# Seven block products for half of the first FFN's down projection, woven between its gate and up products

## The chip, the cores and the metric

The kernel runs on one core of a Trainium2 chip. TensorE (PE) multiplies, VectorE (DVE) and ScalarE (ACT) do the work around the products, GpSimd (POOL) a few small things, and SyncE (SP) issues nearly all transfers from HBM. The metric is the device time of one execution in microseconds, the median over runs; less is better.

## The reference, cut to what matters

A decoder trunk of two layers works on 256 tokens of width 1024, in float32. Each layer is FFN, mixer, FFN; each FFN has 2816 hidden columns and adds half of its result.

```python
def swiglu(x, w_gate, w_up, w_down):
    return (jax.nn.silu(x @ w_gate) * (x @ w_up)) @ w_down

for layer in range(DEPTH):
    h = h + 0.5 * swiglu(rms_norm(h, ffn1_norm[layer]), ...)
    hn = rms_norm(h, mix_norm[layer])
    h = h + (ab_mixer(hn, ...) if layer % 2 == 0 else c_mixer(hn, ...))
    h = h + 0.5 * swiglu(rms_norm(h, ffn2_norm[layer]), ...)
return rms_norm(h, final_norm)
```

The change touches one FFN of the four, the first of layer 0 (`ffn(0)`).

## The kernel before, in words

Everything is kept transposed: a tile holds 128 columns of the model or of the hidden width on its partitions and the 256 tokens along the free axis. A float32 product is made of three matmuls (`mm3`, lines 354 to 356) of parts in fp32r: high x high, high x low, low x high. So each operand is first split into two parts, by a copy on ScalarE (`hi`) and a subtraction on VectorE (`lo`). For x and h that is done once; for the weights it is done for every chunk.

The weights come as one stream of chunks of up to 128 x 2048 floats (1 MB). `weight_chunks` writes their order down, and the class `Stream` runs it: SP loads a chunk into one of 3 raw buffers (line 183), ACT copies it into `whi` (line 231), DVE subtracts into `wlo` (line 238), usually in two halves of 1024 elements, and there are 4 buffers of `whi` and `wlo`. A load may start when the chunk three before it has been split, a split when TensorE is done with the chunk four before it (`room`, `pump`). `SHIFT` puts a chunk 16 elements into its buffer where the weights are the stationary operand; chunks whose weights move have no shift.

An FFN goes through 22 hidden tiles in 11 pairs. Pair p has a gate chunk and an up chunk, called Gp and Up here: 256 hidden columns each, 48 matmuls of 256 columns, one PSUM bank each. After that `gated` makes h of the pair: DVE multiplies the gate by the row of 1/rms (`gs`, line 684), ACT takes silu (line 685), DVE multiplies by up (`hm`, line 687), and `split` makes `hTh` and `hTl` (line 359). In `ffn(0)` the row is made late, from the sums of squares that are formed during the first chunks (lines 446 to 458), and the first two pairs are gated together after G2 (`late = 4`). The down projection then runs for four groups of 256 columns, each in three chunks of 8, 8 and 6 hidden tiles (`DOWN`), with the weights stationary and h moving; after each group `nxt.pair` adds it to x, makes the next stage's x parts, and squares.

The program's order is not the final order on each engine: a planner goes through it and issues on each engine the earliest instruction in program order that its own model of the machine holds to be ready. Queues are then fixed and in order. PSUM has 8 banks.

The last FFN (`ffn(5)`) already makes its down projection by seven block products (Strassen's scheme in Winograd's form) for 9 of its pairs, with h stationary (`hTh`, and sums `hSh`) and 512 weight columns moving.

Of the kernel before, what the change touches and what calls it, by code (L numbers as in the profile page):

```python
# [10 lines left out]
F32 = mybir.dt.float32  # L11
# [34 lines left out]
SPARE = 2  # L46
AHEAD = [(phase, n) for phase in (2, 3) for n in (4, 8, 12, 16)] + [(3, 19)]

MIX1, MIX2 = (4, 5, 6, 7, 0, 1, 2, 3), (0, 1, 2, 3, 4, 5, 6, 7)


def weight_chunks():

    chunks = []

    def add(m, r, n, c0, c1, shift=0, cuts=(), reset=0, summed=False, kind="N"):
        chunks.append((m[:-1], m[-1], r, n, c0, c1, shift, cuts, reset, summed, kind))

    def cols(m, c0, w, cuts=(), reset=0):
        n = CH // w  # L60
        for k in range(0, KD, n):
            add(m, k * 128, n, c0, c0 + w, SHIFT if w == 256 else 0, cuts, reset)

    def ffn(name, layer, last=False, again=(2, 3)):
        first = len(chunks)
        for c in range(0, FF, 256):
            if len(chunks) == 0:
                for k in (0, 4):
                    add((f"{name}_w_gate", f"{name}_w_up", layer), k * 128, 4, c, c + 256, SHIFT,
                        (1, 2, 3) if k else (0.5, 1, 1.5, 2, 3))  # L70
                continue
            for m in ("gate", "up"):
                n = len(chunks)
                cuts = (6,) if first == 0 and n in again else ()
                cols((f"{name}_w_{m}", layer), c, 256, cuts, RESET if n - first in again else 0)
        wd = (f"{name}_w_down", layer)
        if last:
            for i in range(FT // 2):
                add(wd, i * 256, 2, 0, D, kind=LAST[i])
            return  # L80
        for c in range(0, D, 256):
            for k, n in DOWN:
                add(wd, k * 128, n, c, c + 256, SHIFT)

    def mix(m, order, summed=False):
        for k in order[:4:2]:
            add(m, k * 128, 2, 0, D, SHIFT)
        for c in (0, 512):
            add(m, order[4] * 128, 4, c, c + 512, SHIFT, summed=summed and c == 0)

    ffn("ffn1", 0, again=(2,))
    wab = ("ab_w_in", 0)
    cols(wab, 0, 256)
    cols(wab, 512, 256, reset=RESET)
    cols(wab, 1024, 512)
    cols(wab, 2048, 512)
    for c, n in ((1536, RESET), (1792, 0), (256, RESET), (768, RESET)):
        cols(wab, c, 256, reset=n)
    mix(("ab_w_out", 0), MIX1)
    ffn("ffn2", 0, again=(2,))  # L100
    ffn("ffn1", 1, again=())
    wc = ("c_w_in", 0)
    for c in range(4):
        cols(wc, c * 256, 256, reset=RESET if c % 2 else 0)
        cols(wc, 1024 + c * 256, 256, reset=0 if c else RESET)
        if c % 2 == 0:
            cols(wc, 2048 + c * 256, 512)
    mix(("c_w_out", 0), MIX2, True)
    ffn("ffn2", 1, True, again=(2,))
    return chunks  # L110
# [17 lines left out]
class Stream:  # L128
# [12 lines left out]
    def add(self, nk, w, shift, cuts, reset, summed, kind):  # L141

        cuts = (*(cuts or (() if reset else (nk / 2,))), nk)
        j = self.chunks
        self.chunks += 1
        for step in (1, 2) if kind != "N" else (0,):
            if step < 2 or kind == "X":
                if step == 1 and self.wide is None:
                    self.wide = len(self.loads)
                self.loads.append((j, nk, w, loads_of(j), step))  # L150
            self.specs.append((len(self.loads) - 1, j, nk, w, shift, cuts, reset, summed, step, kind))
# [48 lines left out]
    def split_parts(self):  # L200
        u = self.split
        nc = self.nc
        r, j, nk, w, shift, cuts, reset, summed, step, kind = self.specs[u]
        formed = kind == "Z" and step == 1
        raw = self.raws[r] if formed else self.raws.pop(r)
        his, los = (p.tile([128, CH + LINE], F32R, name=m) for p, m in ((self.hi_pool, "whi"), (self.lo_pool, "wlo")))

        h = w // 2
        far = nk * w - reset * h + RESHIFT // LINE * LINE + RESHIFT

        def at(k):
            return int(k * w) - reset * h + shift

        def part(t, k):
            if k >= reset:
                return t[:, at(k) : at(k) + w]
            return Halves(*(t[:, a : a + h] for a in (far + k * h, shift + k * h)))

        self.parts[u] = tuple([part(t, k) for k in range(nk)] for t in (his, los))

        def split(a, r):
            n = r.free_size()
            hi, lo = his[:, a : a + n], los[:, a : a + n]
            if len(r.shape) == 3:
                hi, lo = (t.rearrange("p (k c) -> p k c", k=reset) for t in (hi, lo))
            if self.lead:
                done = nc.vector.tensor_copy(hi, r)
                self.lead()
                self.lead = None
            else:  # L230
                done = nc.scalar.activation(hi, r, AF.Copy)  # L231
            if summed:
                nc.scalar.activation(lo, r, AF.Copy, scale=-1.0)
                src = self.weights[j, : 128 * nk * w].rearrange("(p c) -> p c", p=128)
                c0 = a - shift
                nc.gpsimd.dma_start(lo, src[:, c0 : c0 + n], accum_op=ALU.add)
            else:
                self.made[u] = done, nc.vector.tensor_sub(lo, r, hi.bitcast(F32))  # L238

        if step:  # L240
            q = w // 2
            self.parts[u] = tuple([t[:, i * q : (i + 1) * q] for i in range(4)] for t in (his, los))
            split(0, raw[:, : 2 * q])
            if formed:
                to = raw[:, : 2 * q].rearrange("p (i c) -> p i c", i=2)
                t2 = raw[:, 2 * q : 3 * q]
                first = nc.vector.tensor_sub(to, t2.unsqueeze(1).to_broadcast([128, 2, q]), to)
            yield
            if formed:
                with self.tc.issue_after(first.ins):  # L250
                    split(2 * q, raw[:, 2 * q :])
                nc.vector.tensor_sub(t2, t2, raw[:, 3 * q :])
            else:
                end = 4 * q if step == 1 else 3 * q
                split(2 * q, raw[:, 2 * q : end])
            yield
            self.read += not formed
            self.split += 1
            return
        if reset:  # L260
            r = raw[:, : reset * w].rearrange("p (k c) -> p k c", k=reset)
            split(far, r[:, :, :h])
            split(shift, r[:, :, h:])
        k0 = reset
        for k1 in cuts:
            split(at(k0), raw[:, int(k0 * w) : int(k1 * w)])
            k0 = k1
            yield
        self.read += 1
        self.split += 1  # L270
# [41 lines left out]
def trunk(ctx: ExitStack, tc: tile.TileContext, a, out):  # L312
# [340 lines left out]
    def ffn(phase):  # L653
        nonlocal nxt
        with tc.tile_pool(name="fp", bufs=1) as fp:
            hT = [fp.tile([128, FT, S], F32R, name=n) for n in ("hTh", "hTl")]
            last = phase == 5
            if last:
                size = [128, len(SEVEN), 3, 128]
                early = [fp.tile(size, t, name=n) for t, n in ((F32, "hSh"), (F32R, "hSl"))]  # L660
# [21 lines left out]
            def gated(k, pg, pu):  # L682
# [6 lines left out]
                if seven:  # L689
# [6 lines left out]
                    nc.vector.tensor_sub(a21, a12, s2)  # L696
                    nc.vector.tensor_scalar(a22, a22, -1.0, None, op0=ALU.mult)
                split(hT[0][:, k : k + 2], hT[1][:, k : k + 2], hm)
                if seven:
                    split(*(h[:, SEVEN.index(k // 2)] for h in hS), f[:, :3])  # L700

            late = {0: 4, 3: 2}.get(phase, 3)
            if phase in (2, 5):
                split(*parts[:2], nxt.acc[:, 0])
            for n in range(FT):
# [34 lines left out]
                        gated(i, *ready[i : i + 2])  # L740
                elif n > late and m == 1:
                    gated(k, *ready[-2:])
            if last:
                wide = [xp.tile([128, KD, S], F32, name=m).rearrange("p k s -> p (k s)") for m in ("xTh", "xTl")]
                st.spare.append(wide[0])
# [2 lines left out]
                return  # L748
            row = norm["half"]
            nxt = Next(phase + 1)  # L750
            for c in range(4):
                b = bank()
                for k0, n in DOWN:
                    w = st.take()
                    for kk in range(n):
                        k = k0 + kk
                        for j in range(2):
                            cs = slice(j * 128, (j + 1) * 128)
                            mm3(b[:, j * S : (j + 1) * S], w[0][kk][:, cs], w[1][kk][:, cs], hT[0][:, k], hT[1][:, k],
                                k == j == 0, k == FT - 1 and j == 1)  # L760
                    if k0 + n == FT:
                        nxt.pair(c, b, row, fp)
                    st.free()

    def finish(hT, hS, half, away, xr, xn, fg):

# [539 lines left out]
def _layout(a):  # L1306
# [6 lines left out]
    for j, (ms, layer, r, n, c0, c1, *how) in enumerate(chunks):  # L1313
# [2 lines left out]
            w = w[:, ROWS]  # L1316
        w = tiles(w)
        if how[-1] != "N":
            w = w.reshape(128, 4, -1)[:, [3, 1, 0, 2]]
        w = w.reshape(128, loads_of(j), -1).transpose(1, 0, 2)  # L1320
        weights[j, : w.size] = w.ravel()
    norms = np.stack([a[n] for n in ("ffn1_norm", "mix_norm", "ffn2_norm")]).reshape(-1, 128)
# [34 lines left out]
```

## Time and profile before

| | us |
|---|---|
| median of 3 runs | 924.01 (923.49 to 924.04) |
| span of the profiled execution, first to last instruction | 922.4 |
| the profiled execution's own time beyond its span | not given; the runs' median is 1.6 above the span |
| PE busy | 915.0 (99%) |
| DVE busy | 689.8 (75%) |
| ACT busy | 528.4 (57%) |
| first FFN on PE, up to the first product of the mixer | 185.8 |
| of that, its down projection | 125.95 to 185.79 |

Rows of a timeline give start, length, engine, line and operation, output and inputs, shapes, a count (x2 where rows were merged), and in brackets the idle time before it on its engine and what ended it. PE is pipelined: a matmul takes longer than the distance to the next one's start.

### The profile page before, as it was taken

The page shows a single profiled execution, that of the slowest core. Times are in us where ns is not written, and L with a number is a line of the kernel's source. Part 1 is how long each engine was busy: PE and PEld are TensorE (multiplying, and loading weights), DVE is VectorE, ACT ScalarE, POOL GpSimd, SP SyncE. Part 2 cuts the span into 40 slices and gives each one's busy share as a digit, 9 for nine tenths or more (in the row PEclk, how much of TensorE's full clock was granted, in tenths as well). Part 3 has the DMA queues.
Part 4 walks back from the last instruction along what each step waited for, and adds up shares of the span by engine and source line. Part 5 has one row for each costly group of instructions (what it writes and reads, how often), then busy time and mean ns, then how long its engine had stood idle before and what let it go on. Part 6 is the DMA issues. An engine that isn't in the chain of part 4 may idle for free.

```text
span 922.4 us, 18258 instructions
## 1 busy us (share of the span) xinstructions
PE 915.0 (99%) x7583; PEld 896.5 (97%) x7583; DVE 689.8 (75%) x1058; ACT 528.4 (57%) x808; POOL 80.8 (9%) x117
## 2 busy tenths in 40 slices
PE   9999999999999999999999999999999999999997
PEld 9999999999999999999999999999999999999886
DVE  7976556587888867655677666667778799978897
ACT  7754444468667545444564444455776777555574
POOL 0000000033310000000000000001565100000002
PEclk9999999999999999999999999999999999999999
DMA  9765554665256677766556878865533466855681
GB/s 325 272 228 183 180 195 174 228 226 181 93 183 230 220 281 266 296 238 218 187 209 236 305 272 313 318 216 192 184 137 137 119 230 225 277 191 206 223 310 60
DMA packets 33985, 202.15 MB, mean 219 GB/s; under 512 B 3904, under 2 KB 6208, under 8 KB 12528
## 3 DMA queue, kind: packets, MB, share of 16 engines
q1 hardware_dynamic: 32400, 197.79, 59.8%
q0 software_dynamic: 496, 1.77, 0.9%
q10 hardware_dynamic: 1008, 1.44, 0.5%
q8 instruction: 59, 0.97, 0.4%
q14 instruction: 22, 0.18, 0.1%
HBM read 188.14 MB, written 12.85 MB: 218 GB/s over the span
## 4 chain that ended last, share of the span: by engine, by line
PE 93%; issue 4%; DMA 2%; POOL 0%; DVE 0%; ACT 0%; POOLq 0%; DVEq 0%
PE bank L354 30%; PE bank L355 30%; PE bank L356 30%; DMA raw<-in_weights 1%; PE bank L1059 1%; DMA x<-blocks 1%; PE bank L601 1%; DMA xTl<-away 0%; POOL xTl L803 0%; DVE wlo L238 0%; PE bank L604 0%; PE bank L1021 0%; PE bank L1023 0%; PE bank L1022 0%; PE bank L1208 0%
## 5 line engine op out<-in xcount | busy, mean ns | idle before, releaser
L231 ACT ACTIVATE whi<-raw 128x1024 fp32r<-128x1024 f32 (+5 forms) x349 | 331.6, 994 | 280.4 <-issue 154.6
L238 DVE TENSOR_TENSOR wlo<-raw,whi 128x1024 fp32r<-128x1024 f32 (+5 forms) x349 | 390.6, 1149 | 78.8 <-ACT whi L231 77.8
L354 PE MATMUL bank<-xTh,whi 128*128 128x256 f32 x1600 | 442.7, 277 | 0.0
L356 PE MATMUL bank<-xTh,wlo 128*128 128x256 f32 x1600 | 441.8, 276 | 0.0
L355 PE MATMUL bank<-xTl,whi 128*128 128x256 f32 x1600 | 441.8, 276 | 0.0
L355 PEld LDWEIGHTS bank<-xTl,whi 128*128 128x128 f32 x1600 | 300.4, 188 | 0.0
L354 PEld LDWEIGHTS bank<-xTh,whi 128*128 128x128 f32 x1600 | 300.4, 188 | 0.0
L356 PEld LDWEIGHTS bank<-xTh,wlo 128*128 128x128 f32 x1600 | 300.4, 188 | 0.0
L356 PE MATMUL bank<-hTh,wlo 128*128 128x256 f32 x528 | 145.7, 276 | 0.0
L354 PE MATMUL bank<-hTh,whi 128*128 128x256 f32 x528 | 145.7, 276 | 0.0
L355 PE MATMUL bank<-hTl,whi 128*128 128x256 f32 x528 | 145.7, 276 | 0.0
L355 PEld LDWEIGHTS bank<-hTl,whi 128*128 128x128 f32 x528 | 99.1, 188 | 0.0
L354 PEld LDWEIGHTS bank<-hTh,whi 128*128 128x128 f32 x528 | 99.1, 188 | 0.0
L356 PEld LDWEIGHTS bank<-hTh,wlo 128*128 128x128 f32 x528 | 99.1, 188 | 0.0
L687 DVE TENSOR_TENSOR hm<-gs,bank 128x512 f32<-128x512 f32 x44 | 29.9, 683 | 45.4 <-PE bank L356 44.4
L954 POOL MEMSET k<- 64x256 f32 x12 | 3.2, 307 | 565.2 <-ACT whi L231 378.9
L684 DVE TENSOR_TENSOR gs<-bank,row 128x512 f32<-128x512 f32 x44 | 30.1, 686 | 21.3 <-PE bank L356 21.1
L354 PE MATMUL bank<-mixh,whi 128*128 128x256 f32 x128 | 35.7, 279 | 0.0
L356 PE MATMUL bank<-mixh,wlo 128*128 128x256 f32 x128 | 35.4, 277 | 0.0
L355 PE MATMUL bank<-mixl,whi 128*128 128x256 f32 x128 | 35.4, 276 | 0.0
L1050 POOL TENSOR_SCALAR pr<-pr,rl 128x128 f32<-128x128 f32 (+1 forms) x36 | 31.9, 899 | 29.5 <-DVE rl L1046 20.5
L359 ACT ACTIVATE hTh<-hm 128x512 fp32r<-128x512 f32 x44 | 27.1, 619 | 8.8 <-DVE hm L687 8.0
(231 smaller groups left out, 994.1 us busy)
## 6 DMA issues: line engine op xcount, KB each, us to landing
raw<-in_weights SPq DMA_DIRECT2D x139, 1024.0 KB, 5.0
raw<-in_weights SPq DMA_DIRECT2D x12, 768.0 KB, 4.8
blocks<-in_weights SPq DMA_DIRECT2D x9, 1024.0 KB, 10.0
blocks<-blocks SPq DMA_DIRECT2D x9, 1024.0 KB, 8.7
raw<-blocks SPq DMA_DIRECT2D x7, 1024.0 KB, 4.8
raw<-in_weights SPq DMA_DIRECT2D x6, 512.0 KB, 6.6
raw<-in_weights SPq DMA_DIRECT2D x7, 256.0 KB, 5.7
blocks<-block SPq DMA_DIRECT2D x5, 256.0 KB, 8.9
```

Source lines behind the costliest of these rows:

```text
L231: done = nc.scalar.activation(hi, r, AF.Copy)
L238: self.made[u] = done, nc.vector.tensor_sub(lo, r, hi.bitcast(F32))
L354: nc.tensor.matmul(p, sh, mh, start=start, stop=False)
L355: nc.tensor.matmul(p, sh, ml, start=False, stop=False)
L356: return nc.tensor.matmul(p, sl, mh, start=False, stop=stop)
L359: return nc.scalar.activation(hi, src, AF.Copy), nc.vector.tensor_sub(lo, src, hi.bitcast(F32))
L601: nc.tensor.matmul(o, w[0][i][:, cs], xT[m][:, k], start=k == 0 and m == "h" and j % 2 == 0, stop=False)
L684: nc.vector.tensor_mul(g, both(pg), twice(norm["row"]))
L687: nc.vector.tensor_mul(hm, g, both(pu))
L954: nc.gpsimd.memset(pair[j][o, 1].bitcast(F32), 0.0)
L1050: share = engine.tensor_scalar(pr[:, cs], pr[:, cs], rl[:, b : b + 1], None, op0=ALU.mult)
L1059: nc.tensor.transpose(tp[:, i * 128 : (i + 1) * 128], pr[:, i * 128 : (i + 1) * 128], ident)
```

## The change

For the first FFN (`WOVEN = (0,)`), columns 0 to 511 of the down projection are made by seven block products per pair of h tiles. The pair's h (2 hidden tiles x 256 tokens) is cut into 2 x 2 blocks by hidden tile and by half of the tokens, its weights (2 x 512) into 2 x 2 blocks of 256 columns, and seven products of a block or a sum of blocks replace eight. Called S0 to S10 here, they are woven into the stage: Sp stands behind U(p+2) (`LAG = 2`), S9 behind S8 and S10 behind the first chunk of the third column group. In them h is stationary and the weights move; the seven sums stay in four PSUM banks from S0 to S10.

- The weights of Sp come as one chunk of 128 x 1024 floats, kind `"S"`, put 48 elements into the buffer (`MSHIFT`). DVE forms four sums of blocks in the unused half of the raw buffer (three instructions), and ACT and DVE split seven blocks instead of four.
- `gated` also forms four sums of h blocks on DVE (three instructions) and splits them (`hSh`, `hSl`, three buffers).
- After S10, `gather_first` adds the seven results up into four quarters, with one ACT copy and seven DVE instructions. They have tokens on the partitions, so `turned` transposes them on PE (four 128 x 128 blocks at a time) into a bank, after the second and third chunk of the third group, and hands them to `nxt.pair`. The groups of columns 512 to 1023 are as before.

```diff
+WOVEN = (0,)
+LAG = 2
+MSHIFT = 48
@@ weight_chunks
+        def seven(pair):
+            add(wd, pair * 256, 2, 0, 512, MSHIFT, kind="S")
...
+            if woven and c // 256 >= LAG:
+                seven(c // 256 - LAG)
...
-        for c in range(0, D, 256):
+        rest = list(range(FT // 2 - LAG, FT // 2)) if woven else []
+        if woven:
+            seven(rest.pop(0))
+        for c in range(512 if woven else 0, D, 256):
             for k, n in DOWN:
                 add(wd, k * 128, n, c, c + 256, SHIFT)
+                if rest:
+                    seven(rest.pop(0))
@@ Stream.split_parts
+        if kind == "S":
+            q = w // 2
+            self.parts[u] = tuple([t[:, shift + i * q : shift + (i + 1) * q] for i in range(7)] for t in (his, los))
+            b12, t13, t1, t2, t4 = (raw[:, i * q : j * q] for i, j in ((0, 1), (4, 6), (4, 5), (6, 7), (7, 8)))
+            split(shift, raw[:, q : 4 * q])
+            nc.vector.tensor_add(t13.rearrange("p (i c) -> p i c", i=2),
+                                 raw[:, q : 3 * q].rearrange("p (i c) -> p i c", i=2),
+                                 b12.unsqueeze(1).to_broadcast([128, 2, q]))
+            nc.vector.tensor_add(t2, t1, raw[:, 2 * q : 3 * q])
+            nc.vector.tensor_add(t4, t2, raw[:, 3 * q : 4 * q])
+            yield
+            split(shift + 3 * q, raw[:, 4 * q :])
...
@@ gated
+                if woven:
+                    f = g.rearrange("p i (t c) -> p (i t) c", t=2)
+                    a11, a12 = (hm[:, i, :128] for i in range(2))
+                    nc.vector.tensor_sub(f[:, :2], hm[:, 0].rearrange("p (t c) -> p t c", t=2), hm[:, :, 128:])
+                    nc.vector.tensor_sub(f[:, 2], f[:, 1], a11)
+                    nc.vector.tensor_add(f[:, 3], a12, f[:, 2])
+                    summed[k // 2] = [fp.tile([128, 4, 128], F32R, name=m, bufs=3) for m in ("hSh", "hSl")]
+                    split(*summed[k // 2], f)
@@ ffn
+            def seven_products(c):
+                if not sevens:
+                    sevens.extend(bank() for _ in range(4))
+                w = st.take()
+                plain = [[h[:, 2 * c + k, t * 128 : (t + 1) * 128] for h in hT] for k, t in ((0, 0), (1, 0), (1, 1))]
+                s3, s1, s2, s4 = ([h[:, i] for h in summed[c]] for i in range(4))
+                a11, a12, a22 = plain
+                for i, (at, (sh, sl), q) in enumerate(((0, a11, 0), (1, a12, 2), (2, s4, 1), (3, a22, 6), (4, s1, 3),
+                                                       (5, s2, 5), (6, s3, 4))):
+                    b = sevens[at // 2][:, at % 2 * S : (at % 2 + 1) * S]
+                    mm3(b, sh, sl, w[0][q], w[1][q], c == 0 and at % 2 == 0, c == FT // 2 - 1 and at in (1, 3, 5, 6))
+                st.free()
+                summed.pop(c)
...
+            def gather_first():
+                p1, p2, q3, q4, q5, p6, p7 = (sevens[i // 2][:, i % 2 * S : (i % 2 + 1) * S] for i in range(7))
...
+                nc.scalar.activation(u1, p1, AF.Copy)
+                nc.vector.tensor_add(u2, u1, p6)
+                nc.vector.tensor_add(c11, u1, p2)
+                nc.vector.tensor_add(u3, u2, p7)
+                nc.vector.tensor_add(c21, u3, q4)
+                nc.vector.scalar_tensor_tensor(c22, u3, -1.0, q5, op0=ALU.mult, op1=ALU.add)
+                nc.vector.scalar_tensor_tensor(v, u2, -1.0, q5, op0=ALU.mult, op1=ALU.add)
+                nc.vector.tensor_add(c12, v, q3)
...
+            def turned(i, parts):
+                b = bank()
+                for j in range(2):
+                    for t in range(NT):
+                        at = j * S + t * 128
+                        nc.tensor.transpose(b[:, at : at + 128], parts[t][:, j * 128 : (j + 1) * 128], ident)
+                nxt.pair(i, b, norm["half"], fp)
...
+                if woven and m == 1 and k // 2 >= LAG:
+                    seven_products(k // 2 - LAG)
...
+            rest = list(range(FT // 2 - LAG, FT // 2)) if woven else []
+            if woven:
+                seven_products(rest.pop(0))
-            for c in range(4):
+            for c in range(2 if woven else 0, 4):
...
+                    if woven and c == 2 and k0:
+                        turned(k0 // 16, quarters[k0 // 16])
                     if k0 + n == FT:
                         nxt.pair(c, b, row, fp)
                     st.free()
+                    if rest:
+                        seven_products(rest.pop(0))
+                        quarters = gather_first()
```

More of the change, by code (lines that the diff above doesn't have):

```diff
@@ L62, in cols, with ffn @@
             add(m, k * 128, n, c0, c0 + w, SHIFT if w == 256 else 0, cuts, reset)
-    def ffn(name, layer, last=False, again=(2, 3)):
+    def ffn(name, layer, last=False, again=(2, 3), woven=False):
         first = len(chunks)
+        wd = (f"{name}_w_down", layer)
+        def seven(pair):
+            add(wd, pair * 256, 2, 0, 512, MSHIFT, kind="S")
         for c in range(0, FF, 256):
@@ L75, in ffn @@
                 cols((f"{name}_w_{m}", layer), c, 256, cuts, RESET if n - first in again else 0)
-        wd = (f"{name}_w_down", layer)
+            if woven and c // 256 >= LAG:
+                seven(c // 256 - LAG)
         if last:
@@ L89, in mix @@
             add(m, order[4] * 128, 4, c, c + 512, SHIFT, summed=summed and c == 0)
-    ffn("ffn1", 0, again=(2,))
+    ffn("ffn1", 0, again=(2,), woven=0 in WOVEN)
     wab = ("ab_w_in", 0)
@@ L99, in weight_chunks @@
     mix(("ab_w_out", 0), MIX1)
-    ffn("ffn2", 0, again=(2,))
-    ffn("ffn1", 1, again=())
+    ffn("ffn2", 0, again=(2,), woven=2 in WOVEN)
+    ffn("ffn1", 1, again=(), woven=3 in WOVEN)
     wc = ("c_w_in", 0)
@@ L145, in add @@
         self.chunks += 1
-        for step in (1, 2) if kind != "N" else (0,):
+        for step in (1, 2) if kind in "ZX" else (0,):
             if step < 2 or kind == "X":
@@ L238, in split @@
                 self.made[u] = done, nc.vector.tensor_sub(lo, r, hi.bitcast(F32))
+        if kind == "S":
[10 more added lines that the diff above has]
+            split(shift + 3 * q, raw[:, 4 * q :])
+            yield
+            self.read += 1
+            self.split += 1
+            return
         if step:
@@ L657, in ffn @@
             last = phase == 5
+            woven = phase in WOVEN
             if last:
@@ L699, in gated @@
                 if seven:
                     split(*(h[:, SEVEN.index(k // 2)] for h in hS), f[:, :3])
+            summed, sevens = {}, []
+            def seven_products(c):
[11 more added lines that the diff above has]
+                summed.pop(c)
@@ new lines, in gather_first @@
+            def gather_first():
+                p1, p2, q3, q4, q5, p6, p7 = (sevens[i // 2][:, i % 2 * S : (i % 2 + 1) * S] for i in range(7))
+                t = [fp.tile([128, 2, S], F32, name="gs", bufs=2) for _ in range(2)]
+                t += [fp.tile([128, 2, S], F32, name="hm", bufs=2) for _ in range(2)]
+                (u1, u2), (u3, v), (c11, c21), (c12, c22) = ([v[:, i] for i in range(2)] for v in t)
+                nc.scalar.activation(u1, p1, AF.Copy)
[6 more added lines that the diff above has]
+                nc.vector.tensor_add(c12, v, q3)
+                sevens.clear()
+                return (c11, c21), (c12, c22)
@@ L1318, in _layout @@
         if how[-1] != "N":
-            w = w.reshape(128, 4, -1)[:, [3, 1, 0, 2]]
+            w = w.reshape(128, 4, -1)[:, [1, 0, 3, 2] if how[-1] == "S" else [3, 1, 0, 2]]
         w = w.reshape(128, loads_of(j), -1).transpose(1, 0, 2)
```

## The prediction

> **What bounds the kernel now.** I read the profile page first (shares by engine, then the chain of work that ended last), next the table of stages for the first FFN, and then the timelines of PE, DVE and ACT in that stage.
>
> ```profile
> span 922.4 us, 18258 instructions
> PE 915.0 (99%) x7583; PEld 896.5 (97%) x7583; DVE 689.8 (75%) x1058; ACT 528.4 (57%) x808; POOL 80.8 (9%) x117
> PE 93%; issue 4%; DMA 2%; POOL 0%; DVE 0%; ACT 0%; POOLq 0%; DVEq 0%
> ```
>
> ```profile
> 16.80:28.00 11.20, 11.20 (x101) 11.20 (x100) 10.56 (x14) 9.36 (x14) 0.00 (x0) 1.00 0.82 292
> 28.00:49.80 21.80, 21.80 (x195) 21.80 (x194) 20.26 (x25) 15.53 (x20) 0.00 (x0) 1.00 0.78 283
> 49.80:125.95 76.15, 76.15 (x674) 76.15 (x673) 47.32 (x51) 35.60 (x43) 0.00 (x0) 1.00 0.56 197
> 125.95:185.80 59.85, 59.85 (x531) 59.85 (x530) 36.06 (x42) 27.42 (x35) 0.00 (x0) 1.00 0.53 190
> ```
>
> The chain is TensorE for 93% of the span. In the table of stages the columns are stretch, length, then busy us (and instructions) of PE, PEld, DVE, ACT and POOL, the granted clock, the DMA share and GB/s. From 16.8 to 185.8 us PE is busy for the whole of every stretch, at clock 1.00. So in this FFN a matmul less is time less, as long as nothing else becomes late. DVE is the one to watch: busy 20.26 of 21.80 us from 28.0 to 49.8, only 47.32 of 76.15 in the rest of the gate and up products, 36.06 of 59.85 in the down projection. GpSimd does nothing here.
>
> A busy PE need not be at its peak, so I take its pace from starts.
>
> ```profile
> 27.69 0.28 PE L356 MATMUL bank<-xTh,wlo 128*128 128x256 f32 x1
> 27.80 0.28 PE L446 MATMUL bank<-acch,all_ones 128*128 128x256 f32 x1
> 27.92 0.28 PE L447 MATMUL bank<-accl,all_ones 128*128 128x256 f32 x1
> 28.03 0.28 PE L354 MATMUL bank<-xTh,whi 128*128 128x256 f32 x1
> ...
> 125.95 0.28 PE L354 MATMUL bank<-hTh,whi 128*128 128x256 f32 x1
> ...
> 185.79 0.28 PE L354 MATMUL bank<-xTh,whi 128*128 128x256 f32 x1
> ```
>
> The first row of the down projection starts at 125.95 and the first of the mixer at 185.79. Between them are 22 h tiles x 8 column tiles x 3 matmuls = 528: 59.84/528 = 0.1133 us each, with no gap. One chunk of a gate or up product (48 matmuls) takes 5.44 us: those of pair 2 (G2, U2) run from 28.03 to 38.91, and G3, U3 to 49.8.
>
> **The change part by part.**
>
> *Fewer products (PE).* Half the columns cost 22 x 4 x 3 = 264 matmuls of 256 columns before; now 11 pairs x 7 products x 3 = 231, also of 256 columns. 33 x 0.1133 = -3.74 us. PE changes between the two kinds of stream some 22 times; the rows at 27.80 and 28.03 show such a change, with steps of 0.11 and 0.12, so I take nothing for it.
>
> *Pace of the new products.* In them h is stationary and the weights move. The kernel has such products of 256 columns in its last stage only.
>
> ```profile
> 911.71 0.39 PE L356 MATMUL bank<-whi,hTl 128*128 128x512 f32 x1
> 911.94 0.39 PE L354 MATMUL bank<-whi,hTh 128*128 128x512 f32 x1
> ...
> 913.65 0.28 PE L354 MATMUL bank<-whi,hTh 128*128 128x256 f32 x1
> ...
> 916.05 0.28 PE L356 MATMUL bank<-whi,hTl 128*128 128x256 f32 x1
> ```
>
> ```profile
> 217.81 0.66 PE bank L1059 x6
> ```
>
> From 913.65 to 916.05 are 20 steps of 0.120, not 0.1133, though the 512-column ones keep 0.23 (2 x 0.1133 is 0.227). So the pace depends on something other than shape. Ends for 231 matmuls: 0 and 231 x 0.0067 = +1.55 us. The unshifted weights of the tail start at offset 0 of their buffer; the products above that run at 0.1133 read weights 16 elements further (SHIFT), and the new ones are put 48 further (MSHIFT). As offset is the difference I can see, I take 0. TensorE: Matmul & The Clock Gate in the Trainium skill (Step-by-step, LDWEIGHTS) says that loading the next weights doesn't take read bandwidth from the running matmul, so that one shape would have one pace and this term could only be 0; the tail's 0.120 disagrees, which is why I keep the upper end.
>
> *Turning the sums back.* Eight 128x128 transposes are new, in two groups of four. The chain has six of L1059's in 0.66 us (last row above): 0.11 each, +0.88 us.
>
> *VectorE: weights.* ACT and DVE split every chunk into two parts.
>
> ```profile
> 36.03 1.23 DVE L238 TENSOR_TENSOR wlo<-raw,whi 128x1024 fp32r<-128x1024 f32 x1 [0.67 <-ACT whi L231]
> 37.17 0.42 DVE L452 SCALAR_TENSOR_TENSOR sqrt<-sqrt,mean 128x256 f32<-128x256 f32 x1
> 37.51 1.22 DVE L238 TENSOR_TENSOR wlo<-raw,whi 128x1024 fp32r<-128x1024 f32 x1
> 38.64 0.42 DVE L454 SCALAR_TENSOR_TENSOR row<-sqrt,inverse 128x256 f32<-128x256 f32 x1
> 39.09 1.29 DVE L684 TENSOR_TENSOR gs<-bank,row 128x512 f32<-128x512 f32 x2
> 40.50 1.23 DVE L238 TENSOR_TENSOR wlo<-raw,whi 128x1024 fp32r<-128x1024 f32 x1
> 42.44 1.28 DVE L687 TENSOR_TENSOR hm<-gs,bank 128x512 f32<-128x512 f32 x2 [0.72 <-ACT gs L685]
> 43.64 0.69 DVE L684 TENSOR_TENSOR gs<-bank,row 128x512 f32<-128x512 f32 x1
> 44.24 1.22 DVE L238 TENSOR_TENSOR wlo<-raw,whi 128x1024 fp32r<-128x1024 f32 x1
> 45.38 1.28 DVE L359 TENSOR_TENSOR hTl<-hm,hTh 128x512 fp32r<-128x512 f32 x2
> ...
> 47.18 1.22 DVE L238 TENSOR_TENSOR wlo<-raw,whi 128x1024 fp32r<-128x1024 f32 x1
> 48.32 0.68 DVE L359 TENSOR_TENSOR hTl<-hm,hTh 128x512 fp32r<-128x512 f32 x1
> 48.92 1.21 DVE L238 TENSOR_TENSOR wlo<-raw,whi 128x1024 fp32r<-128x1024 f32 x1
> ```
>
> From start to start: 1.14 for 1024 elements (44.24 to 45.38), 0.60 for 512 (43.64 to 44.24), 0.34 for 256 (37.17 to 37.51); by the same slope about 0.87 for 768 and 0.21 for 128. An S chunk (one pair's share of 512 columns) costs three sums (512, 256, 256: 1.28) and splits of 768 and 1024 (2.01): 3.3 us of DVE. A pair's h sums cost 0.34 + 0.21 + 0.21 and a split of 512, 0.60: 1.36 us. ACT gets three copies more, under 2.5 us per pair, beside 35.60 busy of 76.15.
>
> In the steady part DVE has 47.32 us per 7 pairs now, 6.8 per pair; then 6.8 + 3.3 + 1.36 = 11.4 us, while PE takes 10.88 + 2.38 = 13.26 per pair. 86%: hidden, if lookahead keeps its order.
>
> *The pinch.* Between 28.0 and 49.8 DVE is 93% busy, and S0, S1 and the sums of pairs 0 and 1 fall into just this stretch. G4, due at 49.8 now, comes due at 49.8 + 2 x 2.38 = 54.55. By then DVE must do what it does now to 49.8 (20.26), less the four 1024-wide splits at 40.50, 44.24, 47.18 and 48.92, which are for U4 and G5 (4.56), plus S0 and S1 (6.6), plus two pairs' sums (2.7): 25.0 us of 26.55. With pair 2's sums too it is 26.4. Now it idles 1.54 us there. So it ends between 1.5 us early and 1.4 us late; I take 0.6 us of PE waiting. Cover for it would be G4's present lead: its split ends at 38.7, used at 49.8, 11 us, and all of that is spent. Later points gain 1.9 us per pair, so the wait is paid once.
>
> *PSUM.* Four of eight banks are held from S0 to the gather. G and U keep four, so G(p+2) needs the bank of G(p) read; between are U, S, G, U, S = 21 us. Nothing.
>
> *DMA.* The bytes are the same; five more loads pass SP's queue, but two half-size ones come ahead of G3 and G4.
>
> ```profile
> 34.94 2.01 ACT L231 ACTIVATE whi<-raw 128x1024 fp32r<-128x1024 f32 x2 [1.85 <-DMA raw<-in_weights]
> 39.42 1.05 ACT L231 ACTIVATE whi<-raw 128x1024 fp32r<-128x1024 f32 x1
> 40.48 1.28 ACT L685 ACT_TABLE_LOAD   x1
> 43.78 1.14 ACT L359 ACTIVATE hTh<-hm 128x512 fp32r<-128x512 f32 x2
> ```
>
> ACT waited 1.85 us for G4's weights at 34.94, 15 us ahead of their use; with S0's split in front of it, it is asked for later than that. Hidden.
>
> *Gather and end of phase.* The gather's eight short DVE operations (0.34 to 0.42) have one chunk's 48 matmuls (5.44 us) beside them before the first turn; the first turn needs five of them, about 2 us. Pairs 0 and 1 of x are then updated in the third quarter, long before pair 3, which still ends the phase. 0, or 0.5 us if DVE is in a split.
>
> Sum: -3.74 + 0 + 0.88 + 0.6 = -2.26. The profiled execution's span is 922.4, the median of the runs 924.0, 1.6 more around it; the change lies inside, and PE's chain behind shifts as a whole. 924.0 - 2.3 = **921.8 us**.
>
> **The rivals.**
>
> *S0 stands too early in PE's queue (slower).* S0 is traced right behind U2, which ends at 38.91. But pair 0's h needs the row (38.64), the table load (40.48), hm (42.44) and hTl, done at 46.7; with S0's split ahead (3.3) in place of G4's (2.3), and the sums, 48 to 49. If PE's queue had S0 right behind U2, PE would stand 9 to 10 us: 924.0 - 2.9 + 9.5 = 930.6. Behind G3 and U3 it costs nothing, since they end at 49.8. It turns slower when less than some 56 of their 96 matmuls (6.4 us) stand in front. For the late place:
>
> ```profile
> 893.58 0.39 PE L354 MATMUL bank<-whi,hTh 128*128 128x512 f32 x1
> 893.80 0.39 PE L354 MATMUL bank<-whi,hSh 128*128 128x512 f32 x1
> 894.03 0.39 PE L354 MATMUL bank<-whi,hTh 128*128 128x512 f32 x1
> 894.26 0.39 PE L355 MATMUL bank<-wlo,hTh 128*128 128x512 f32 x1
> ```
>
> The code issues L354, L355, L356 in turn; here three L354 come first, without a gap. So the planner puts PE work that it thinks ready ahead of work that it thinks late. What speaks against it: its own clock may be off by some us. 0.14, center 927.
>
> *The pinch is wider.* If operations cost DVE their durations (0.69, 1.22) and not their steps (0.60, 1.14), 0.085 more on some 43 instructions (25 in the row, 18 new) is 3.6 us, so PE waits 1.5 to 4 us: 922.7 to 925.3. Against: the rows' starts. For: ACT must copy before each split, and DVE is at 94 to 99%. VectorE: DVE Perf Modes in the Trainium skill (The DRAIN you can't avoid) states that the next operation starts only when the pipe of the one before is empty; by that rule it would be this case, but starts 0.60 apart under a 0.69 duration don't bear it out. 0.20, center 923.6.
>
> *The 0.120 pace.* All 231 at it: 921.8 + 1.5 = 923.3, within 0.2%. 0.10.
>
> That the matmuls don't fall is no case: their count follows from the loops.
>
> **How the numbers follow.** Forecast 0.51 (921.0 to 922.2), a little better 0.05 (no wait at all: 920.9 to 921.1), the three rivals 0.20, 0.10, 0.14. A measurement here can tell about 0.2%, 1.85 us. Faster (under 922.2): 0.56. Within: 0.30 of the two middle rivals and 0.02 of the first, 0.32. Slower: 0.12. Range 920.9 to 926.0: what it leaves out is most of the first rival (0.10) and a little below (0.04).
>
> **What would show it.** PE matmuls fall by 33 less 8 transposes: 7558 in all (7583 now). The new products' starts are 0.113 apart, or 0.120 if that rival holds. The mixer's first xTh product starts 2.3 us earlier than 185.79. In the stages DVE is near full from 28 to 66 us and about 86% from there to 150. PE shows idle, if any, once, at G4 or at the first S product, released by DVE; over 3 us of it at S0 means the first rival, several such idles up to 120 us that DVE's cost is mis-sized.

## The result, and the profile after

The changed kernel takes **932.48 us** (median; 931.79 to 933.14) where the kernel before takes 924.02 (923.49 to 924.13): a ratio of 1.0093, 95% interval 1.0078 to 1.0107. It is slower by 8.5 us; the forecast was 921.8. What came is the first rival: S0 stands in PE's queue ahead of G3 and U3, and PE waits there.

The page of the changed kernel (first lines):

```profile
span 930.6 us, 18340 instructions
PE 915.5 (98%) x7558; PEld 896.7 (96%) x7558; DVE 729.4 (78%) x1152; ACT 544.5 (59%) x830; POOL 80.5 (9%) x117
```

The matmuls fell to 7558 as counted, and PE's busy time didn't. The table by stretch shows where (columns as in the prediction; the 0.50 and 0.84 are the granted clock; the second row is a part of the first):

```profile
28.00:49.80 21.80, 14.37 (x109) 13.88 (x108) 20.30 (x34) 12.05 (x16) 0.00 (x0) 0.84 0.53 204
48.00:49.00 1.00, 1.00 (x7) 1.00 (x6) 1.00 (x2) 0.29 (x1) 0.00 (x0) 0.50 0.00 0
49.80:100.00 50.20, 50.20 (x441) 50.20 (x441) 44.37 (x64) 29.36 (x36) 0.00 (x0) 1.00 0.55 189
```

Only the stretch from 28.0 to 49.8 lost anything: PE, busy for all of it before, is busy 14.37 of 21.80 us. From 49.8 on PE is full again. What it waited for (us, times, longest):

```profile
PE bank L385 <- ACT hTh L390: 7.4, 1, 7.4
```

And PE's timeline (line 385 is line 354 of before; the last bracket is the idle time and what ended it):

```profile
27.12 0.28 PE L477 MATMUL bank<-acch,all_ones 128*128 128x256 f32 x1
...
38.11 0.28 PE L387 MATMUL bank<-xTh,wlo 128*128 128x256 f32 x1
45.76 0.58 PE L385 MATMUL bank<-whi,hTh 128*128 128x256 f32 x1 [7.37 <-ACT hTh L390]
...
48.07 0.41 PE L387 MATMUL bank<-whi,hTl 128*128 128x256 f32 x1
48.28 0.41 PE L385 MATMUL bank<-whi,hTh 128*128 128x256 f32 x1
...
51.04 0.28 PE L387 MATMUL bank<-xTh,wlo 128*128 128x256 f32 x1
...
74.62 0.28 PE L385 MATMUL bank<-whi,hTh 128*128 128x256 f32 x1
...
77.12 0.28 PE L385 MATMUL bank<-xTh,whi 128*128 128x256 f32 x1
...
193.28 0.28 PE L385 MATMUL bank<-xTh,whi 128*128 128x256 f32 x1
```

U2's last matmul starts at 38.11; the next in the queue is S0's first, on pair 0's h, at 45.76. Behind it PE runs at half clock: from 46.99 on starts are 0.21 apart, up to 49.7; the three steps ahead of that are longer still. From 45.76 to 51.04 it does 25 matmuls of S0 and S1 (all 21 of S0, and four of S1 drawn forward) and two of G3. Why pair 0's h comes then, from the timelines of DVE and ACT:

```profile
31.82 2.96 ACT L246 ACTIVATE whi<-raw 128x1024 fp32r<-128x1024 f32 x3 [1.39 <-DMA raw<-in_weights]
...
40.22 0.41 DVE L485 SCALAR_TENSOR_TENSOR row<-sqrt,inverse 128x256 f32<-128x256 f32 x1
...
44.01 1.28 DVE L719 TENSOR_TENSOR hm<-gs,bank 128x512 f32<-128x512 f32 x2
...
45.09 1.14 ACT L390 ACTIVATE hTh<-hm 128x512 fp32r<-128x512 f32 x2
...
48.82 0.68 DVE L390 TENSOR_TENSOR hSl<-gs,hSh 128x512 fp32r<-128x512 f32 x1
```

The norm's row is made at 40.22, hm at 44.01, hTh, which S0's first matmul waits for, from 45.09, and the last part of pair 0's sums from 48.82. Some 1.1 us of this is a load: ACT waits 1.39 us for weights at 31.82, where in sums_aligned, with S0 at the same place, it waits 0.30 at 30.70; there the row is made at 39.09 and PE waits 5.9 us.

The ledger, from starts. From the sum of squares to the mixer's first product: 185.79 - 27.80 = 157.99 us before, 193.28 - 27.12 = 166.16 after, +8.17 (the spans differ by 8.2). Terms: 33 matmuls fewer, -3.74; transposes, +0.72; an S is 77.12 - 74.62 = 2.50 us for 21 matmuls, 0.119 each, where 21 x 0.1133 is 2.38: 11 x 0.12 = +1.32; the wait, 45.76 - 38.22 = +7.54; the 27 matmuls in 5.28 us where 3.20 is their pace at full clock, +2.08 (some 0.6 of it lies in the first three steps, 45.76 to 46.99, which 0.21 a step does not explain). Sum +7.92; 0.25 us is left over.

### The profile page after: what moved, and what is told of

The parts are those of the page before. It is cut to its first block, busy times and chain, and to the rows that moved or that the text cites. A ratio compares the mean times of both kernels' runs of the same rounds, so it can differ in the third digit from the quotient of the medians.

```text
span 930.6 us, 18340 instructions
## 1 busy us (share of the span) xinstructions
PE 915.5 (98%) x7558; PEld 896.7 (96%) x7558; DVE 729.4 (78%) x1152; ACT 544.5 (59%) x830; POOL 80.5 (9%) x117
## 4 chain that ended last, share of the span: by engine, by line
PE 89%; issue 4%; DMA 4%; DVE 2%; ACT 1%; POOL 0%; SPq 0%; POOLq 0%; DVEq 0%; ACTq 0%
PE bank L385 29%; PE bank L387 29%; PE bank L386 29%; DMA raw<-in_weights 2%; DVE wlo L253 1%; PE bank L1152 1%; DMA x<-blocks 1%; ACT whi L246 1%; DMA xTl<-away 0%; POOL xTl L896 0%; PE bank L1116 0%; PE bank L1114 0%; PE bank L1115 0%; PE bank L1301 0%; DVE gs L716 0%
## 5 line engine op out<-in xcount | busy, mean ns | idle before, releaser
L246 ACT ACTIVATE whi<-raw 128x1024 fp32r<-128x1024 f32 (+5 forms) x359 | 340.3, 991 | 244.3 <-PE bank L386 125.2
L253 DVE TENSOR_TENSOR wlo<-raw,whi 128x1024 fp32r<-128x1024 f32 (+5 forms) x359 | 401.4, 1145 | 58.7 <-ACT whi L246 57.7
L385 PE MATMUL bank<-hTh,whi 128*128 128x256 f32 x440 | 121.6, 276 | 0.0
L386 PE MATMUL bank<-hTl,whi 128*128 128x256 f32 x440 | 121.5, 276 | 0.0
L387 PE MATMUL bank<-hTh,wlo 128*128 128x256 f32 x440 | 121.5, 276 | 0.0
L386 PEld LDWEIGHTS bank<-hTl,whi 128*128 128x128 f32 x440 | 82.6, 188 | 0.0
L385 PEld LDWEIGHTS bank<-hTh,whi 128*128 128x128 f32 x440 | 82.6, 188 | 0.0
L387 PEld LDWEIGHTS bank<-hTh,wlo 128*128 128x128 f32 x440 | 82.6, 188 | 0.0
L717 ACT ACTIVATE gs<-gs 128x512 f32<-128x512 f32 x44 | 27.3, 622 | 16.2 <-DVE gs L716 16.2
L385 PE MATMUL bank<-whi,hTh 128*128 128x256 f32 (+1 forms) x81 | 27.8, 343 | 7.4 <-ACT hTh L390 7.4
```

What stands on the lines that cost most here:

```text
L385: nc.tensor.matmul(p, sh, mh, start=start, stop=False)
L386: nc.tensor.matmul(p, sh, ml, start=False, stop=False)
L387: return nc.tensor.matmul(p, sl, mh, start=False, stop=stop)
L717: nc.scalar.activation(g, g, AF.Silu)
```

## The experiments

Times of before beside them differ a little from chip to chip; each ratio is against the runs of its own chip.

**Place in the queue.** Theory Q: S0's place is the cause. Rivals: VectorE's added work, or the sevens' cost wherever they stand.

s0_behind_u3 (S0 and S1 both behind U3; four buffers for the sums; S0's weights move in the stream in the same way, in lines not shown):

```
-                if woven and m == 1 and k // 2 >= LAG:
-                    seven_products(k // 2 - LAG)
+                if woven and m == 1 and k // 2 > LAG:
+                    for c in (0, 1) if k // 2 == LAG + 1 else (k // 2 - LAG,):
+                        seven_products(c)
```

> S0 is moved from behind U2 to behind U3 (S0 and S1 then stand together there; one buffer more for the h sums); all else as in the changed kernel. Theory Q (the loss is S0's place in PE's fixed queue): pair 0's h is there at about 46 us and U3 ends at 49, so the wait of 7.4 us and the slow matmuls after it (2.5 us) go: 932.5 - 9.9 = 922.6, between 922.0 and 923.6. Theory D (DVE has too much to do, so PE waits wherever S0 stands): over 928, with PE idle at S0, S1 or G4 instead.

Measured: 922.97 us against 923.70, 0.9992 (0.9982 to 1.0001). Its waits of PE, its stretches and its timeline:

```profile
PE bank L609 <- PEq L1439: 0.8, 1, 0.8
```

```profile
28.00:49.80 21.80, 21.80 (x195) 21.80 (x194) 21.77 (x36) 15.14 (x20) 0.00 (x0) 1.00 0.52 186
49.80:100.00 50.20, 50.20 (x440) 50.20 (x440) 48.58 (x72) 31.15 (x39) 0.00 (x0) 1.00 0.61 221
```

```profile
27.51 0.28 PE L478 MATMUL bank<-acch,all_ones 128*128 128x256 f32 x1
...
49.50 0.28 PE L386 MATMUL bank<-whi,hTh 128*128 128x256 f32 x1
...
54.49 0.28 PE L386 MATMUL bank<-xTh,whi 128*128 128x256 f32 x1
65.37 0.28 PE L386 MATMUL bank<-whi,hTh 128*128 128x256 f32 x1
...
164.08 0.60 PE L783 MATMUL bank<-ident,hm 128*128 128x128 f32 x4
164.44 0.37 PE L386 MATMUL bank<-hTh,whi 128*128 128x256 f32 x1
...
184.03 0.28 PE L386 MATMUL bank<-xTh,whi 128*128 128x256 f32 x1
```

```profile
41.11 0.63 ACT L391 ACTIVATE hTh<-hm 128x512 fp32r<-128x512 f32 x1 [0.21 <-DVE hm L720]
```

PE is full through both stretches and waits for none of the new work, although DVE is busy 21.77 of 21.80 us. The mixer starts 184.03 - 27.51 = 156.52 us behind the sum of squares, 1.47 less than before; the terms without the wait give -3.74 + 0.72 + 1.32 = -1.70. (The medians differ by only 0.73 us; the profiled execution took 922.57, one of the fastest.) Theory Q holds; neither rival does. But the place is more than PE's queue: with S0's weights later in the stream DVE's order changes too, the norm's row is made at 37.14 in place of 40.22 (39.09 without the late load), and pair 0's hTh from 41.11 in place of 45.09 (last row). S0's early place made PE wait, and it stood beside a later h. The four transposes of one group take 0.36 us (164.08 to 164.44), 0.09 each.

s0_behind_g3 (S0 between G3 and U3, its weights in the stream too, in lines not shown):

```
+                if woven and m == 0 and k // 2 == LAG + 1:
+                    seven_products(0)
-                if woven and m == 1 and k // 2 >= LAG:
+                if woven and m == 1 and k // 2 > LAG:
```

> S0 stands behind G3, so half of the products that could cover the wait stand in front of it; all else as in the changed kernel. Theory Q: 5.4 us of the 7.4 us wait are covered, 2.0 us are left, too short for the clock to fall: about 932.5 - 5.4 - 2.5 = 924.6, between 923.8 and 927. Theory D: as the changed kernel, over 930.

Measured: 923.75, 1.0002 (0.9993 to 1.0012), just under the range expected: with 48 matmuls in front S0 has 0.2 us left to wait, not 2.0.

```profile
PE bank L387 <- ACT hSh L392: 0.2, 1, 0.2
```

```profile
41.99 1.23 ACT L392 ACTIVATE hTh<-hm 128x512 fp32r<-128x512 f32 x2 [0.40 <-DVE hm L721]
```

Pair 0's hTh is made from 41.99, 3.1 us earlier than in the changed kernel. Both shortened the wait, the 5.4 us of matmuls in front and the earlier h. So the prediction's break-even of 56 matmuls, reckoned with h at 48 to 49, was near by luck.

**What the place costs.** Two runs leave S0 where the change put it.

s0_on_x (for pair 0 alone, S0's held blocks are blocks of x, which are ready):

```
+                if c == 0:
+                    x = [[xT[m][:, k, t * 128 : (t + 1) * 128] for m in "hl"] for k in range(4) for t in range(2)]
+                    plain, (s3, s1, s2, s4) = x[:3], x[3:7]
```

> The changed kernel with S0 at its place behind U2, but the held blocks of S0's 21 matmuls (and of no other S) are blocks of the normalized x, which lie ready, in place of pair 0's h and its sums; pair 0's h and sums are still formed, and S0's results are not the reference's. Theory Q (the place in the queue costs only because pair 0's h comes late): the 7.4 us wait and the slow products behind it go, so that the time is that of s0_behind_u3, 922.9 us (922.0 to 924.2; 0.4 us more for each G,U of 96 products that should fall into the slow rhythm). Rival B (the place itself costs, by S0's weights or by banks that G3 lacks, whatever S0 multiplies): a wait of several us stays ahead of S0 or of G3: 927 to 932 us. Rival C (the clock fell for another reason than the wait, so that it falls here too): the granted clock from 28 to 50 us is 0.84 again and the time 924.5 to 925.5 us.

Measured: 928.08 against 923.80, 1.0046 (1.0031 to 1.0062). Theory Q in this narrow form is wrong; rival B has a part. PE's timeline:

```profile
38.67 0.28 PE L385 MATMUL bank<-whi,xTh 128*128 128x256 f32 x1
...
41.12 0.39 PE L385 MATMUL bank<-whi,xTh 128*128 128x256 f32 x1 [0.87 <-DVE gs L716]
...
43.97 0.58 PE L385 MATMUL bank<-xTh,whi 128*128 128x256 f32 x1 [1.55 <-DVE hm L719]
...
56.59 0.28 PE L385 MATMUL bank<-whi,hTh 128*128 128x256 f32 x1
```

```profile
44.00:47.00 3.00, 3.00 (x14) 3.00 (x15) 3.00 (x9) 3.00 (x5) 0.00 (x0) 0.50 0.02 5
```

S0 stops after 12 matmuls, which fill two banks, until gs has read a gate's bank; G3 stops until hm has read an up's. Pairs 0 to 2 hold six of the eight PSUM banks until the row (here at 39.44) lets them be read, and S0 asks for four. Waits 2.42 us, G3 and U3 12.62 us in place of 10.88 (the first of them at a granted clock of 0.50, last row), S0's rest 0.4: 4.5 us. From 28 to 50 us the clock is 0.92, not rival C's 0.84, but it does fall, behind waits of only 0.87 and 1.55 us. By difference, then, and as an estimate from two runs whose rows were made 0.8 us apart, pair 0's late h is some 5 of the 9.6 us that S0's place cost (7.54 + 2.08), and banks with the clock behind them would have cost the rest had h been early. Both hang on when the row is made.

kept_warm (36 fp32 products of zeros ahead of S0, to hold the clock up):

```
+                for _ in range(36 if c == 0 else 0):
+                    nc.tensor.matmul(sevens[3][:, S : S + 128], zero, zero, start=True, stop=True)
```

> 36 float32 products of zeros are put ahead of S0 (into the unused half of the fourth of its banks), so that PE works through the wait; nothing else. If the slow matmuls after the wait (0.21 us instead of 0.113) are the clock falling during it: they run at 0.113 and 932.5 falls by up to 2.5 us, to about 930.2. If they are slow because the sums come late from DVE: 932.5, with gaps in their place. More than 933.5 would mean that the zeros take longer than the wait.

Measured: 931.67, 1.0089 (1.0073 to 1.0104): 0.8 us under the changed kernel's 932.48, a third of what was expected, and 0.5 us when each is taken against before on its own chip. The two intervals overlap, so a gain is not established. Its stretch and timeline:

```profile
28.00:49.80 21.80, 21.21 (x187) 21.00 (x186) 21.30 (x35) 13.31 (x18) 0.00 (x0) 1.00 0.59 217
```

```profile
46.53 0.37 PE L385 MATMUL bank<-whi,hTh 128*128 128x256 f32 x1
...
48.46 0.39 PE L387 MATMUL bank<-whi,hSl 128*128 128x256 f32 x1 [0.59 <-DVE hSl L390]
```

```profile
47.73 0.68 DVE L390 TENSOR_TENSOR hSl<-gs,hSh 128x512 fp32r<-128x512 f32 x1
```

The clock stays at 1.00, but behind the zeros S0 starts at 46.53, and then it waits for the sums. In the changed kernel the slow clock lay beside that same lateness: hSl was made from 48.82 on. Here it is made from 47.73, 1.1 us earlier, as no load was late (0.24 us of waiting at 30.72). That alone could be the 0.8. So the 2.08 us of slow clock were worth 0.8 at most here, and perhaps nothing.

**The new products' pace.** The changed kernel's S matmuls take 0.119 on average: some 0.117 ahead of a block of h itself, 0.120 ahead of a sum. I suspected addresses (in SBUF, of the program as built): their moving weights start 192 B past a multiple of 256 B, the sums held next 32 B past one, 96 B further on (modulo 256, as are all distances here); G and U have 64 B there and take 0.113.

sums_aligned (sums moved by a wider tile in front, so that they too stand 64 B on; the working tiles gs and hm, which PE does not read in these products, move with them):

```
-        nc.scalar.activation(fp.tile([128, 1], F32, name="first"), warm[:, :1], AF.Copy)
+        nc.scalar.activation(fp.tile([128, 64], F32, name="first")[:, :1], warm[:, :1], AF.Copy)
```

> A tile of 4 bytes ahead of the h sums in SBUF is made 256 bytes wide, so that the sums start at a multiple of 256 bytes and not 32 bytes past one; nothing else. Theory A (the 0.120 us of the products with hSh and hSl come from their address): 132 matmuls go from 0.120 to 0.113, 932.5 - 0.9 = 931.6, and S0's wait stays. If the pace has another cause: 932.5, and the steps stay 0.120.

Measured: 934.74, 1.0121 (1.0105 to 1.0136): a miss, on the wrong side. Its timeline:

```profile
62.71 0.28 PE L385 MATMUL bank<-xTh,whi 128*128 128x256 f32 x1
73.60 0.28 PE L385 MATMUL bank<-whi,hTh 128*128 128x256 f32 x1
76.08 0.28 PE L385 MATMUL bank<-xTh,whi 128*128 128x256 f32 x1
87.39 0.29 PE L385 MATMUL bank<-whi,hTh 128*128 128x256 f32 x1
89.79 0.28 PE L385 MATMUL bank<-xTh,whi 128*128 128x256 f32 x1
```

S itself does fall, from 2.50 to 2.40 us (87.39 to 89.79). But a G and U, which nothing was done to, takes 10.89 us up to 73.60 and 11.31 from 76.08: 0.1178 a matmul, at clock 1.00 and with no wait. So products with the 64 B distance have two paces, 0.113 and 0.118. The next five runs, all with S0 behind U3, look for what chooses.

u3_sums_at_64 (`MSHIFT = 0`, `first` 16 wide), u3_sums_aligned (`first` 64 wide) and u3_sums_at_192 (`MSHIFT = 32`, `first` 48 wide): sums 64 B on, at three moving addresses.

> S0 behind U3 as in s0_behind_u3 (922.97 us), and the addresses of the S products moved: their weights, which move through PE, start at a multiple of 256 B (before at 192 past one), and the h sums, which are held, 64 B past one (before 32 past). In the S groups of sums_aligned and of the G and U groups the held block lay 64 B behind the start of the moving one, and such products took either 113 or 118 ns; at other distances 117 to 122 ns. Theory P (two rhythms at a distance of 64 B, one for each moving address; a group whose moving address fits the rhythm takes 113 ns, the other 118): G, U and the twelve products on sums have the same moving address here, so both run at 113 ns; nine products on h itself stay at 120. S takes 12 x 0.1133 + 9 x 0.120 = 2.44 us in place of 2.50, G and U stay at 10.89 us for 96, and the time is 11 x 0.06 = 0.7 us below s0_behind_u3: 922.3 us (921.7 to 922.9). Theory N (the slower G and U of sums_aligned had nothing to do with moving addresses): some groups of 96 take 11.30 us again, up to nine of them, 0.4 us each: up to 926.

> S0 behind U3, and the h sums at a multiple of 256 B as in sums_aligned (held block 64 B behind the moving one in all S products, moving address 192 past a multiple of 256 B). Theory P (two rhythms, one for each moving address): either S takes 2.41 us and G and U 11.30 us for 96, or S 2.50 and G and U 10.89; which of them holds can change where S and G meet: between 923.0 (never in the slow rhythm) and 923.0 + 9 x 0.41 - 11 x 0.09 = 925.7 us; taken: 925. Theory L (the slow rhythm in sums_aligned came from the 5.9 us wait ahead of S0, which is gone here): G and U stay at 10.89 throughout, S takes 2.41 to 2.50 us: 922.0 to 923.0 us.

> S0 behind U3; the moving weights of the S products start 128 B past a multiple of 256 B, the h sums 192 B past one: a distance of 64 B with a third moving address, while the nine products on h itself have a distance of 128 B (122 ns where it occurs in the trace). Theory P: the sums' products run in a rhythm that need not be that of G and U: G and U 10.89 or 11.30 us for 96, S 9 x 0.122 + 12 x 0.1133 to 0.118 = 2.46 to 2.51: 922.6 to 926.3 us. Theory N (moving addresses don't matter, distances do): S 2.46 us as the distance of 64 B gives it, G and U as in u3_sums_at_64, and the same time as that run but for 11 x 0.02 = 0.2 us.

Measured against 924.15: 926.28, 1.0023 (1.0014 to 1.0032); 926.45, 1.0025 (1.0015 to 1.0035); 926.12, 1.0021 (1.0012 to 1.0030). In u3_sums_at_64:

```profile
54.71 0.28 PE L386 MATMUL bank<-xTh,whi 128*128 128x256 f32 x1
66.02 0.28 PE L386 MATMUL bank<-whi,hTh 128*128 128x256 f32 x1
```

From 54 us on every G and U takes 11.30 or 11.31 us, in all three, the first with G's own moving address. Theory P is wrong, and so is L: no wait stands in front here. Theory N, that the moving address doesn't matter, is left: the three times lie within 0.4 us. All three have S end 64 B on.

u3_plain_last (as s0_behind_u3; the product on h22, 64 B on, moved to the end of S):

```
-(2, s4, 1), (3, a22, 6), (4, s1, 3), (5, s2, 5), (6, s3, 4)
+(2, s4, 1), (4, s1, 3), (5, s2, 5), (6, s3, 4), (3, a22, 6)
```

> s0_behind_u3 with one edit: in each S the product on h22 itself (held block 64 B behind the moving one) stands last, behind the three on sums (96 B behind), where it stood fourth. Theory E (the distance at the end of S sets the rhythm of the G and U that follow: 64 B leaves them at 118 ns, another distance puts them at 113): G and U go from 10.89 to 11.30 us for 96, nine times or so, and the time to 922.97 + 9 x 0.41 = 926.6 us (925.5 to 927.5). Theory A (most of S at 64 B is what does it, wherever it stands): G and U stay at 10.89 and the time at 922.97 us (922.4 to 923.8).

Measured: 926.01 against 923.80, 1.0025 (1.0016 to 1.0034).

```profile
55.14 0.28 PE L386 MATMUL bank<-xTh,whi 128*128 128x256 f32 x1
66.45 0.29 PE L386 MATMUL bank<-whi,hTh 128*128 128x256 f32 x1
```

11.31 us, with the same products in another order: theory A is wrong, E held.

u3_lo_apart (`first` 64 wide, and a 32 B tile between the sums' high and low halves, so that only the low ones stand 96 B on):

> s0_behind_u3 with the two halves of the h sums at different distances from the moving weights: the high halves (two of each three matmuls) 64 B behind, the low halves (the last of each three, and so the last of S) 96 B behind, as in s0_behind_u3. Theory E (what stands at the end of S sets the rhythm of the G and U behind it; only a 64 B end leaves them at 118 ns): G and U stay at 10.89 us for 96, and of S's twelve matmuls on sums eight stand at 64 B; if those take 113 to 118 ns in place of 120, S falls from 2.50 to between 2.43 and 2.49 and the time is 0.1 to 0.8 us below s0_behind_u3: 922.5 us (921.8 to 923.2). Theory A (most of S at 64 B is what does it): G and U 11.30 us, 926.3 us.

Measured: 925.04 against 924.16, 1.0011 (1.0002 to 1.0020).

```profile
55.23 0.28 PE L386 MATMUL bank<-xTh,whi 128*128 128x256 f32 x1
66.54 0.29 PE L386 MATMUL bank<-whi,hTh 128*128 128x256 f32 x1
69.01 0.28 PE L386 MATMUL bank<-xTh,whi 128*128 128x256 f32 x1
79.92 0.28 PE L386 MATMUL bank<-whi,hTh 128*128 128x256 f32 x1
82.39 0.28 PE L386 MATMUL bank<-xTh,whi 128*128 128x256 f32 x1
93.70 0.29 PE L386 MATMUL bank<-whi,hTh 128*128 128x256 f32 x1
```

11.31, then 10.91, then 11.31 again, in turn through the phase, and a time 2.5 us above the one expected. Theory E is too simple as well: the same end of S leaves either pace. That one S after another switches it looks like a state with two values which some products flip; that is a guess, and it stays open.

u3_sums_at_96 (as s0_behind_u3; `first` 24 wide: sums 160 B on), run twice:

> s0_behind_u3 with the h sums at 96 past a multiple of 256 B in place of 32: a distance of 160 B to the moving address, which no product of the kernels so far has. Theories E and A both have G and U at 10.89 us for 96 here, as no S ends at 64 B. S's twelve products on sums take 113 to 122 ns, the ends that other distances showed, against 120: the time is 922.97 us and 11 x 12 x (-0.007 to +0.002), so 922.0 to 923.3 us; taken: 922.9.

> The same kernel as u3_sums_at_96, on the chip of u3_lo_apart, so that the two stand against the same runs of before: 922.5 us again, 1.0 to 1.4 us under before, if that difference was no chance of the runs; 923.0 (the time of s0_behind_u3, whose products have the same pace) if it was.

Measured: 922.49 against 923.80, 0.9988 (0.9980 to 0.9997), and 922.91 against 924.16, 0.9987 (0.9978 to 0.9995).

```profile
54.60 0.28 PE L386 MATMUL bank<-xTh,whi 128*128 128x256 f32 x1
65.50 0.28 PE L386 MATMUL bank<-whi,hTh 128*128 128x256 f32 x1
67.99 0.28 PE L386 MATMUL bank<-xTh,whi 128*128 128x256 f32 x1
```

G and U at 10.90, S at 2.49: the paces of s0_behind_u3, whose interval overlaps. This version is faster than both kernels, by 1.3 us against before on either chip, both intervals below 1; whether it beats s0_behind_u3 isn't told apart.

## Why the prediction was wrong

- **The step that failed: S0's place.** The forecast put S0 behind G3 and U3, on the argument that the planner puts work that it thinks ready ahead of work that it thinks late. The row shown for it was three high products drawn forward within the last stage; it shows that matmuls are reordered, not that a whole S would give way to G3. The plan put the first 16 matmuls of S0 and S1, and then the rest of S0, ahead of nearly all of G3, and PE stood 7.4 us for pair 0's hTh; with S0 behind U3 that wait is gone and the kernel takes 922.97. "Its own clock may be off by some us" was the right doubt, and 0.14 too little for it. Why the plan stands so was not shown.
- **The rival's price.** 9 to 10 us of standing; measured 7.54 of wait and 2.08 of slow clock, 9.6. The sum fits by luck: h came 2 to 3 us earlier than reckoned (hTh at 45.7, not 48 to 49), and the clock was not priced. The table has clock 0.50 in the stretch from 48 to 49 us, and starts stay 0.21 apart to 49.7. TensorE: Matmul & The Clock Gate in the Trainium skill (Part 1: The HAM clock gate) says that PE falls to half clock after an idle window of some 3.4 us and needs about as long of work to come back; the trace agrees, with 7.4 us of idleness and 3.9 us of work at 0.50. In s0_on_x less was enough: the clock fell to 0.50 behind waits of 0.87 and 1.55 us with 1.3 us of matmuls between them.
- **PSUM, "nothing".** Wrong at the start of the phase. That G and U keep four banks holds once h flows; until the row comes, pairs 0 to 2 hold six, and s0_on_x shows 2.42 us of waits for banks at S0's early place. Behind U3 the term is nothing.
- **Pace of the new products.** I took 0, with the upper end +1.55; it was +1.32. The argument, that the weights' own offset sets it, does not hold: MSHIFT of 0, 32 and 48 gave an S of 2.46 to 2.50 us, and with 48 kept the sums' address alone took it to 2.40 (u3_sums_aligned, with G and U slower). The rival of the 0.120 pace was right in its step.
- **Transposes.** +0.88 foretold, +0.72 measured.
- **The pinch.** +0.6 foretold; no wait at G4 in the changed kernel, where PE's standing gave DVE time, and none in s0_behind_u3, whose DVE is full. The rival of a wider pinch falls with it. In the changed kernel's next stretch DVE has 44.37 of 50.20 us, 88%, against the 86% reckoned.
- **Products, -3.74.** Held.

With S0 late the right terms give -1.70, and -1.47 was measured from PE's starts: even in its own case the forecast of -2.26 was 0.8 us too good. Pace alone is 1.32 of it; the pinch that did not come (0.6) and the cheaper transposes (0.16) give part of that back, and 0.23 is left unexplained.

## What to carry to other kernels

When work is woven into a stream, ask of its first instance when its input is made, by the rows of the trace, and put enough of the stream in front by hand; here S0 behind the 48 matmuls of G3 took the kernel from 8.5 us above before to 0.05, also because the inputs came earlier. A start-up stage has its own books: what is read late holds its banks too. And price an idle PE with the half clock behind it (2.08 us here), but expect less back where the next input is late anyway (0.8 at most in kept_warm).

## What was unexpected of the hardware

In these runs the pace of 256-column products goes with the SBUF address of the next held block against that of the moving one. At 96 and 160 B on (modulo 256) it is about 0.120. At 64 B on it is 0.113 or 0.118 for whole groups of 96 matmuls, and the products in front of a group can switch it: in u3_plain_last their order alone did. What switches it inside the engine is open. Moving the sums by 224 B took the kernel from 0.7 us under before (s0_behind_u3) to 2.3 above (u3_sums_aligned, on another chip against its own before), with no wait shown and the clock at 1.00.
